# Mamba scan layer of a decoder trunk: output products for two groups at a time, and a group's scale spread by transfers through memory

## The chip, the cores and the metric

The kernel runs on one core of a Trainium2 chip. The metric is the device time of one execution, in microseconds (us). A core has five engines with an instruction queue each, which run in order and wait for each other by semaphores: PE multiplies matrices (PEld is its weight loading), DVE and ACT do element-wise work and can read PSUM, POOL does element-wise work on SBUF, SP only issues transfers. PE writes to PSUM, here eight banks of 128 x 512 floats: three "mm" banks, three "aux" and two "side".

## What is computed

A trunk of four residual layers over 512 tokens of 1024 channels, all float32: attention, a gated FFN, a Mamba-2 scan layer, and a second gated FFN. The change is in the scan layer:

```python
zxbcdt = h @ w_in                       # z, x, B, C of 8 groups, and dt
xbc = jax.nn.silu(causal_depthwise_conv(xbc, conv_w, conv_b))
y = ssd_chunked_scan(xs, dt, a, bm, cm) # per group: 4 heads of 64, state 128, chunks of 128 tokens
y = y + d_skip * xs
g = y * silu(z)                         # then per group of 256 channels:
g = g * lax.rsqrt(jnp.mean(g * g, axis=-1, keepdims=True) + NORM_EPS)
x = x + (g * norm_w) @ w_out            # 8 groups x 256 channels -> 1024
```

## The kernel before, in words

Channels lie on the partitions and the 512 tokens along a row, so an activation of 128 channels is one 128 x 512 tile. Every weight and activation is split into a high and a low part, and a product of a 128 x 128 weight tile is three matmuls (`mm3`: high by high, high by low, low by high); a "product" below is one such matmul. A weight unit is 128 x 1024 floats: a transfer brings it into a `raw` tile (four buffers), ACT casts it to `hi`, and DVE (POOL for z) subtracts to `lo`; `hi` and `lo` have five buffers each. A unit's buffers are free when PE has done its last product with them.

The scan layer goes over the eight groups g in a loop of three parts i = 0, 1, 2. While the scan of group g runs, PE fills the time with the six projections of group g+1 (x0, b, c, x1, z0, z1: 24 products each, into an mm bank, which DVE reads once, `us...<-...,rbc`, L656) and with output products for earlier groups (`write_groups`, "wso"). A scan is a generator, `scan_group`: decays; transposes and the C*B product (px, pb, pc); states (pst); products and outputs (py, pf, then yt, and on ACT the squares whose sum on DVE is `gsq`); then the norm. For the norm, PE sums the squares over the partitions (`ss`), DVE adds epsilon (`ms`, L201), POOL raises to the power -1/2 (`rg`, 128 x 4, a token's scale on its partition, L202). PE then spreads rg so that every partition has all 512 scales in a row (`along_free`, four float32 products with the identity that show as eight matmuls, tile `prg`, L209), and DVE multiplies the group's two y tiles by it (L805), ACT casts them to high (`y..h`, L807) and DVE subtracts to low (`y..l`, L809).

`write_groups(gs, ys)` makes eight steps, one for each 128 output channels m; a step is 6 products for every group in gs, summed in one mm bank, and then one DVE add into the residual tile xr[m] (L830). Before, the gs are [0,1], [2,3], [4], [5,6] and, at the end, [7].

PE's order is the order of the program here (`manual_schedule`): `between(g)` lists what fills group g's loop, `behind(g)` advances the scans, and `last_rows` writes out the end, where the first products of the next FFN (`part`) are set between the last output steps. The order on DVE, ACT, POOL and SP is made by a scheduler with its own estimate of times, and `queued(name)` ties an instruction to stand behind a given one on its engine.

Of the kernel before, what the change touches and what calls it, by code (L numbers as in the profile page):

```python
# [27 lines left out]
NSG = 8  # L28
# [9 lines left out]
C_GN = C_FIN + KD  # L38
# [13 lines left out]
def trunk(ctx: ExitStack, tc: tile.TileContext, A, out):  # L52
    nc = tc.nc
    V, SC, G, T = nc.vector, nc.scalar, nc.gpsimd, nc.tensor
    dma = nc.sync.dma_start
# [20 lines left out]
    def t2(name, tag, bufs, pool=k2, dtype=F32):  # L76
        return pool.tile([P, 512], dtype, tag=tag, name=name, bufs=bufs)
# [16 lines left out]
    rbc = cp.tile([P, S], F32, tag="rbc", name="rbc")  # L94
# [8 lines left out]
    def col(c):  # L103
        return par[:, c : c + 1]
# [100 lines left out]
    def along_free(r, name, bank=aux_bank):  # L205

        p = bank(name)
        for j in range(r.shape[-1]):
            T.matmul(  # L209
                p[:, j * P : (j + 1) * P], r[:, j : j + 1].to_broadcast([P, P]), ident,  # L210
                start=True, stop=True,
            )
        return p
# [132 lines left out]
    def qk_steps(h):  # L346
        steps = [lambda g=g, c=c: qk_step(h, g, c) for g in range(NG) for c in range(2)]
        return steps + [lambda: v0_step(h)]
# [126 lines left out]
    def wo_first(m):  # L475
        hi, lo = load_unit(A["wo"][m], f"wo{m}")
        p = mm_bank(f"wo{m}") if m < 3 or m > 4 else (aux_bank, side_bank)[m - 3](f"wo{m}")
        for h in range(NH - 1):
            mm3(p, hi, lo, h, oh[h], ol[h], h == 0, False)
        wo_held[m] = (hi, lo, p)  # L480
# [3 lines left out]
    for h in range(NH):  # L484
        if h < NH - 1:
            fill = qk_steps(h + 1)
            if h == NH - 2:
                fill.pop()
        else:
            fill = qk_steps(h)[-1:] + [lambda m=m: wo_first(m) for m in range(3)]  # L490
# [14 lines left out]
    lp = ctx.enter_context(tc.tile_pool(name="lp", bufs=1, reuse_waits="tile"))  # L505
    xr = [lp.tile([P, S], F32, tag=f"xr{k}", name=f"xr{k}") for k in range(KD)]
# [7 lines left out]
    for m in range(KD):  # L514
        if m not in wo_held:
            wo_first(m)
        hi, lo, p = wo_held[m]
# [3 lines left out]
            op=ALU.add  # L521
# [66 lines left out]
    def cst(name):  # L588
        return lp.tile([P, P], F32, tag=name, name=name)

    dtt, adt, acs, dec, cdec = (cst(n) for n in ("dtt", "adt", "acs", "dec", "cdec"))
    rows = tc.dram_tile([NSH, S], F32, name="rows")
    dt3, dec3, cd3 = c3(dtt), c3(dec), c3(cdec)

    def decay_rates():
# [51 lines left out]
    latest = {}  # L647

    def queued(name):
        return tc.issue_after(latest.pop(name).ins) if name in latest else nullcontext()  # L650

    def ssm_tile(i, c_conv, name):
        p = project(A["win"][i], name, V if c_conv is not None else G)
        us = t2("us" + name, *(("a", 13) if c_conv is None else ("us", 3)), lp)
        with queued("mean"):
            V.tensor_tensor(us, p, rbc, op=ALU.mult)  # L656
        if c_conv is None:
            with queued("decay"):
                latest["gate"] = SC.activation(us, us, AF.Silu)
            return us  # L660
        a = t2("a" + name, "a", 13, lp)
        conv(a, us, C_SCW + c_conv * 4, C_SCB + c_conv, 4)
        with queued("decay"):
            SC.activation(a, a, AF.Silu)
        return a
# [16 lines left out]
    def scan_group(g, d, ys):  # L682
# [116 lines left out]
        yield  # L799
        rg = sm.tile([P, 4], F32, tag="rg", name="rg")  # L800
        latest["mean"] = inv_rms(sq0, 2 * P, rg, bank=side_bank)
        yield
        prg = along_free(rg, "prg")
        for x, y in enumerate((y0, y1)):
            V.scalar_tensor_tensor(y, y, col(C_GN + 2 * g + x), prg, op0=ALU.mult, op1=ALU.mult)  # L805
            ys.append(high_low(f"y{g}{x}"))
            SC.copy(ys[-1][0], y)  # L807
        for y, (y_h, y_l) in zip((y0, y1), ys[-2:]):
# [4 lines left out]
    def write_groups(gs, ys):  # L813

        units = {}

        def load(i):
            if i not in units:
                units[i] = [load_unit(A["wso"][2 * g + i], f"wso{g}{i}") for g in gs]

        def step(m):
            i, at = divmod(m, 4)
            load(i)
            p = mm_bank(f"wso{gs[0]}{m}")
            n = 2 * len(gs)
            for c in range(n):
                hi, lo = units[i][c // 2]
                mm3(p, hi, lo, at * 2 + c % 2, *ys[2 * gs[0] + c], c == 0, c == n - 1)
            with queued("mean"):
                V.tensor_tensor(xr[m], xr[m], p, op=ALU.add)  # L830
            if gs[-1] == NSG - 1:
                prep(m, xr[m], C_FFN + KD, ssum_b)

        def timed(m):
            f = lambda: step(m)
            f.products = 6 * len(gs)
            return f

        return load, [timed(m) for m in range(KD)]

    ys = []
    tiles = [{} for _ in range(NSG)]
    ahead = [project_group(g, tiles[g]) for g in range(NSG)]

    w01, w23, w4, w56 = (write_groups(gs, ys)[1] for gs in ([0, 1], [2, 3], [4], [5, 6]))
    scans = [scan_group(g, tiles[g], ys) for g in range(NSG)]

    def behind(g):

        for i in range(3):  # L850
            late = g in (1, 2)
            if late and i == 2:
                next(scans[g - 1], None)
            next(scans[g])
            if g and i == (1 if late else 0) or g > 2 and i == 1:
                next(scans[g - 1], None)
            yield

    def between(g):

        if g < NSG - 1:
            x0, b, c, x1, z0, z1 = ahead[g + 1]
        if g < NSG - 3:
            after = ahead[g + 2][0]
            return [
                [[b, c], [x1, z0], [z1, after]],
                [[b, c], [x1, z0], [z1, after]],
                [[b, c], [x1, z0], [z1, after, *w01[:2]]],
                [[b, w01[2], c], [x1, w01[3], z0], [z1, after, *w01[4:6]]],
                [[b, w01[6], c], [x1, w01[7], z0], [z1, after, *w23[:2]]],  # L870
            ][g]
        if g == NSG - 3:
            return [b, w23[2], c], [x1, w23[3], z0], [z1, *w23[4:6]]
        if g == NSG - 2:
            return [x0, b], [c, x1], [z0, *w23[6:]]
        return [*w4[:4], ahead[g][5]], [*w4[4:], *w56[:2]], w56[2:4]

    def groups():
        decays = decay_rates()
        next(decays)  # L880
        for i, f in enumerate(ahead[0]):
            f()
            if i == 1:
                next(decays)
        next(decays, None)
        ahead[1][0]()
        next(scans[0])
        for g in range(NSG):
            for i, (_, fill) in enumerate(zip(behind(g), between(g))):
                for j, f in enumerate(fill):  # L890
                    f()
                    if i == 2 and j == 0 and g < NSG - 1:
                        next(scans[g + 1])

    def last_rows():

        scan = scans[-1]
        load7, w7 = write_groups([7], ys)
        next(scan)
        w56[4]()
        load7(0)
        load7(1)
        units = []

        def unit(i):
            name = f"u1_{i}"  # L910
            units.append((
                load_unit(A["wup"][44 + i], name), side_bank(name) if i in (1, 2) else mm_bank(name), name
            ))

        def part(i, *ks):
            if i == len(units):
                unit(i)
            (hi, lo), t, _ = units[i]
            for k in ks:
                mm3(t, hi, lo, k, xh[k], xl[k], k == 0, k == KD - 1)  # L920

        unit(0)
        with tc.manual_schedule(engines={mybir.EngineType.DVE, mybir.EngineType.Activation}):
            next(scan, None)
            for m in range(5, KD):
                w56[m]()
        for m in range(5):
            w7[m]()
        part(0, 0)
        w7[5]()  # L930
        part(0, 1)
        part(1, 0)
        w7[6]()
        part(0, 2)
        part(1, 1)
        part(2, 0)
        w7[7]()
        for k in range(3, KD + 2):
            for i in range(3):
                if k - i < 5:  # L940
                    part(i, k - i)
        for k in range(5, KD):
            for i in range(3):
                part(i, k)
        inv_rms(ssum_b, D, rcol)
        part(3, *range(4))
        p = along_free(rcol, "rb")
        SC.copy(rbc, p)
        part(3, *range(4, KD))
        for _, t, name in units:  # L950
            early[name] = t
# [142 lines left out]
```

## Time and profile before

| | us |
|---|---|
| median of 3 runs | 1669.96 (1669.91 to 1670.53) |
| the profiled execution | 1668.99 |
| its span, first to last instruction | 1667.2 |
| PE busy | 1648.6 |
| DVE busy | 1072.1 |
| ACT busy | 665.4 |
| POOL busy | 464.3 |
| scan layer in the span, about | 880 to 1315 |

In a timeline row the first number is the start in us from the span's start, the second the duration, then engine, line, operation, output<-inputs, the shape and how many; a bracket at the end tells how long the engine sat idle before it and who ended that. In a row of waits stand the total, how many, and the longest. Rows of the chain of waits have start, duration, engine, tile and line. In a table by stretches each engine has its busy time, with the number of instructions in brackets. Rows of transfers end with the median time from issue to landing.

### The profile page before, as it was taken

To read this page: it belongs to the slowest core of one execution; us is meant where nothing else is said; L and a number is where in the kernel's file an instruction comes from. 1 tells how busy PE (TensorE), PEld (TensorE's weight loads), DVE (VectorE), ACT (ScalarE), POOL (GpSimd) and SP (SyncE) were. 2 spreads that over 40 slices of the span, in tenths; PEclk is the share of its full clock that TensorE was granted. 3 is DMA by queue.
4 is the path that set the end of the run, shared out by engine and by line. 5 is a ranking of instruction groups with operands and counts; after the bars stand their busy time and mean duration, and the time that the engine had idled before them with its cause. 6 is when DMAs were issued, how large, how long until landed. Compare 5 with 4: busy or idle time off the path is not lost.

```text
span 1667.2 us, 21490 instructions
## 1 busy us (share of the span) xinstructions
PE 1648.6 (99%) x8230; PEld 1400.2 (84%) x8230; DVE 1072.1 (64%) x1796; ACT 665.4 (40%) x1000; POOL 464.3 (28%) x303
## 2 busy tenths in 40 slices
PE   9999999999999999999999999999989999999997
PEld 8888888888888888888888888888878888888887
DVE  5366555366658745745666888887787684574565
ACT  5233332333244423433445545454443542342345
POOL 0443443144404210220232232333230331121023
PEclk9999999999999999999999999999999999999999
DMA  7322222222223323233233333322332232332323
GB/s 252 102 77 75 82 84 89 89 76 89 76 89 127 101 88 114 90 100 101 76 114 116 102 101 102 114 75 103 101 102 78 87 113 88 102 101 89 110 74 120
DMA packets 52342, 165.56 MB, mean 99 GB/s; under 512 B 5840, under 2 KB 8144, under 8 KB 52240
## 3 DMA queue, kind: packets, MB, share of 16 engines
q1 hardware_dynamic: 51152, 163.15, 29.6%
q8 instruction: 65, 1.06, 0.3%
q10 hardware_dynamic: 1088, 1.05, 0.2%
q14 instruction: 37, 0.30, 0.1%
HBM read 162.01 MB, written 2.16 MB: 98 GB/s over the span
## 4 chain that ended last, share of the span: by engine, by line
PE 87%; DVE 7%; ACT 3%; issue 2%; DMA 1%; POOL 0%; SPq 0%; POOLq 0%; ACTq 0%; DVEq 0%
PE u L127 28%; PE qk L127 15%; PE wd L127 12%; PE v L127 8%; PE wso L127 4%; PE z L127 3%; PE xs L127 3%; PE wz L127 2%; PE wo L127 2%; DVE axs L529 1%; PE b L127 1%; PE c L127 1%; PE pp L416 1%; PE pg L429 1%; PE po L424 1%
## 5 line engine op out<-in xcount | busy, mean ns | idle before, releaser
L127 PE MATMUL u<-xl,hi_u 128*128 128x512 f32 x704 | 270.0, 384 | 0.4 <-DVE xl L176 0.4
L127 PE MATMUL u<-xh,hi_u 128*128 128x512 f32 x704 | 270.4, 384 | 0.0
L127 PE MATMUL u<-xh,lo_u 128*128 128x512 f32 x704 | 270.0, 384 | 0.0
L551 POOL TENSOR_TENSOR au<-au,au 128x512 f32<-128x512 f32 x43 | 56.7, 1320 | 427.0 <-DVE au L529 406.4
L118 ACT CAST hi_u<-raw_u 128x1024 fp32r<-128x1024 f32 x88 | 91.1, 1043 | 193.9 <-PE u L127 102.1
L529 DVE SCALAR_TENSOR_TENSOR au<-usu,par,au 128x510 f32<-128x510 f32 (+1 forms) x176 | 160.8, 918 | 5.9 <-ACT au L527 1.0
L331 POOL TENSOR_TENSOR rotqk<-rotqk,sr 32x512 f32<-32x512 f32 x48 | 91.9, 1914 | 258.1 <-DVE rotqk L330 215.0
L127 PEld LDWEIGHTS u<-xl,hi_u 128*128 128x128 f32 x704 | 131.9, 187 | 25.9 <-DVE xl L176 0.8
L127 PEld LDWEIGHTS u<-xh,lo_u 128*128 128x128 f32 x704 | 131.9, 187 | 25.4
L127 PEld LDWEIGHTS u<-xh,hi_u 128*128 128x128 f32 x704 | 131.9, 187 | 25.2
L127 PE MATMUL qk<-xh,hi_qk 128*128 128x512 f32 x384 | 149.3, 389 | 0.0
L127 PE MATMUL qk<-xl,hi_qk 128*128 128x512 f32 x384 | 148.4, 387 | 0.0
L127 PE MATMUL qk<-xh,lo_qk 128*128 128x512 f32 x384 | 147.2, 383 | 0.0
L544 DVE TENSOR_TENSOR usu<-u,rbc 128x512 f32<-128x512 f32 x88 | 60.5, 690 | 113.3 <-PE u L127 103.9
L119 DVE TENSOR_TENSOR lo_u<-raw_u,hi_u 128x1024 fp32r<-128x1024 f32 x88 | 110.8, 1264 | 24.2 <-ACT hi_u L118 24.2
L564 DVE TENSOR_TENSOR xr<-xr,wd 128x512 f32<-128x512 f32 x40 | 27.3, 687 | 116.8 <-PE wd L127 116.8
L327 DVE TENSOR_TENSOR qk<-qk,cr 128x512 f32<-128x512 f32 x48 | 33.0, 688 | 91.5 <-PE qk L127 91.3
L118 ACT CAST hi_qk<-raw_qk 128x1024 fp32r<-128x1024 f32 x48 | 50.2, 1045 | 100.4 <-PE v L127 50.0
L127 PEld LDWEIGHTS qk<-xh,lo_qk 128*128 128x128 f32 x384 | 72.0, 187 | 13.4
L127 PEld LDWEIGHTS qk<-xh,hi_qk 128*128 128x128 f32 x384 | 72.0, 188 | 13.0
L118 ACT CAST hi_wd<-raw_wd 128x1024 fp32r<-128x1024 f32 (+1 forms) x56 | 52.3, 952 | 76.7 <-PE wd L127 39.7
L127 PEld LDWEIGHTS qk<-xl,hi_qk 128*128 128x128 f32 x384 | 72.1, 188 | 12.5
(636 smaller groups left out, 3931.1 us busy)
## 6 DMA issues: line engine op xcount, KB each, us to landing
raw_u<-in_wup SPq DMA_DIRECT2D x88, 512.0 KB, 3.2
raw_qk<-in_wqk SPq DMA_DIRECT2D x48, 512.0 KB, 3.2
raw_wd<-in_wdn SPq DMA_DIRECT2D x32, 512.0 KB, 3.2
raw_wd<-in_wdn SPq DMA_DIRECT2D x24, 384.0 KB, 2.9
raw_xs<-in_win SPq DMA_DIRECT2D x16, 512.0 KB, 3.3
raw_z<-in_win SPq DMA_DIRECT2D x16, 512.0 KB, 3.6
lm<-rows SPq DMA_DIRECT2D x32, 256.0 KB, 5.9
raw_wso<-in_wso SPq DMA_DIRECT2D x16, 512.0 KB, 3.2
```

The source lines that it names most:

```text
L118: SC.copy(hi[:, s], raw[:, s])
L119: low.tensor_tensor(lo[:, s], raw[:, s], hi.bitcast(F32)[:, s], op=ALU.subtract)
L127: T.matmul(in_turns(dst), w, in_turns(x), start=first, stop=last)
L327: V.tensor_tensor(at(t), of(p), of(cr), op=ALU.mult)
L331: G.tensor_tensor(rot[R, :], rot[R, :], sr[R, :], op=ALU.mult)
L416: T.transpose(pp[:, b * P : (b + 1) * P], pr[:, b * P : (b + 1) * P], ident)
L424: T.matmul(po[:, ii], v0[h][:, b * P : (b + 1) * P], pts[i][:, (b - i + 1) * P : (b - i + 2) * P], start=b == max(i - 1, 0), stop=b == i,)
L429: T.matmul(pg[:, ii], vt[g, half][i][:, es], pts[i][:, (g + 1) * P : (g + 2) * P], start=g == 1, stop=g == 2,)
L529: V.scalar_tensor_tensor(dst[:, j:], src[:, : S - j], col(c_w + taps - 1 - j), dst[:, j:], op0=ALU.mult, op1=ALU.add,)
L544: V.tensor_tensor(us, p, rbc, op=ALU.mult)
L551: by.tensor_tensor(ab[1], ab[0], ab[1], op=ALU.mult)
L564: V.tensor_tensor(xr[m], xr[m], p, op=ALU.add)
```

## The change

Output steps take two groups throughout: [0,1], [2,3], [4,5], and [6,7] at the end; the steps of [4] and [7] alone (6 products) and of [5,6] are gone. The places of the steps in the last loops move with that: two of [2,3] move from loop 6 to loop 7, and loop 7 has three steps of [4,5] in part 1 and two in part 2, with the rest in `last_rows`.

For the groups 0 to 6, rg no longer goes over PE. A transfer from SP writes its 128 x 4 values to a row of `scales` in DRAM in the order of tokens (element by element: neighbours in the row come from neighbouring partitions), and a second transfer reads the row back to all 128 partitions as `prg` in SBUF. The second waits for the first. Group 7 still uses `along_free`. The sum of squares `ss` moves in groups 0 and 1 from behind the states to behind the C*B product, as it already stood for the later groups. The multiplication by the scale (L813 after) is tied on DVE to stand behind the last copy or add made before it in the program.

```diff
+    scales = tc.dram_tile([NSG, S], F32, name="scales")
...
         latest["mean"] = inv_rms(sq0, 2 * P, rg, bank=side_bank)
-        yield
-        prg = along_free(rg, "prg")
+        if g < NSG - 1:
+            dma(scales[g].rearrange("(j t) -> t j", t=P), rg)
+            prg = t2("prg", "prg", 1, lp)
+            dma(prg, scales[g : g + 1, :].to_broadcast([P, S]))
+            yield
+        else:
+            yield
+            prg = along_free(rg, "prg")
         for x, y in enumerate((y0, y1)):
-            V.scalar_tensor_tensor(y, y, col(C_GN + 2 * g + x), prg, op0=ALU.mult, op1=ALU.mult)
+            with queued("copy"):
+                V.scalar_tensor_tensor(y, y, col(C_GN + 2 * g + x), prg, op0=ALU.mult, op1=ALU.mult)
...
-    w01, w23, w4, w56 = (write_groups(gs, ys)[1] for gs in ([0, 1], [2, 3], [4], [5, 6]))
+    w01, w23, w45 = (write_groups(gs, ys)[1] for gs in ([0, 1], [2, 3], [4, 5]))
...
         if g == NSG - 3:
-            return [b, w23[2], c], [x1, w23[3], z0], [z1, *w23[4:6]]
+            return [b, c], [x1, w23[2], z0], [z1, *w23[3:5]]
         if g == NSG - 2:
-            return [x0, b], [c, x1], [z0, *w23[6:]]
-        return [*w4[:4], ahead[g][5]], [*w4[4:], *w56[:2]], w56[2:4]
+            return [x0, b], [c, x1], [z0, w23[5]]
+        return [*w23[6:], ahead[g][5]], w45[:3], w45[3:5]
...
-            for i, (_, fill) in enumerate(zip(behind(g), between(g))):
+            for i, fill in enumerate(between(g)):
+                next(scans[g])
+                if g and i == 0:
+                    next(scans[g - 1])
                 for j, f in enumerate(fill):
                     f()
+                    if g and i == 1 and j == 0:
+                        next(scans[g - 1], None)
...
-        load7, w7 = write_groups([7], ys)
+        load67, w67 = write_groups([6, 7], ys)
         next(scan)
-        w56[4]()
-        load7(0)
-        load7(1)
+        w45[5]()
+        load67(0)
...
-            for m in range(5, KD):
-                w56[m]()
-        for m in range(5):
-            w7[m]()
+            for m in range(6, KD):
+                w45[m]()
+        for m in range(4):
+            w67[m]()
```

Three places of the new order are used below, all on DVE. Names carry the group or step and a buffer number; the change adds 8 to L830 (L838) and to L805, L807 and L809 (L813, L815, L817), and 1 to the lines between.

Loop 3, between the norm's `ms` of group 2 and the projection c of group 4, before:

```order
L201 TENSOR_SCALAR ms_8336<-ss_8331 128x4
L656 TENSOR_TENSOR usb4_8370<-b4_8345,rbc_98 128x512
L529 SCALAR_TENSOR_TENSOR ab4_8372<-usb4_8370,par_76,ab4_8372 128x511
L529 SCALAR_TENSOR_TENSOR ab4_8372<-usb4_8370,par_76,ab4_8372 128x510
L830 TENSOR_TENSOR xr2_4044<-xr2_4044,wso02_8378 128x512
L529 SCALAR_TENSOR_TENSOR ab4_8372<-usb4_8370,par_76,ab4_8372 128x509
L656 TENSOR_TENSOR usc4_8423<-c4_8398,rbc_98 128x512
```

and after:

```order
L201 TENSOR_SCALAR ms_8333<-ss_8328 128x4
L657 TENSOR_TENSOR usb4_8370<-b4_8345,rbc_98 128x512
L529 SCALAR_TENSOR_TENSOR ab4_8372<-usb4_8370,par_76,ab4_8372 128x511
L529 SCALAR_TENSOR_TENSOR ab4_8372<-usb4_8370,par_76,ab4_8372 128x510
L838 TENSOR_TENSOR xr2_4044<-xr2_4044,wso02_8378 128x512
L529 SCALAR_TENSOR_TENSOR ab4_8372<-usb4_8370,par_76,ab4_8372 128x509
L813 SCALAR_TENSOR_TENSOR yt_8141<-yt_8141,par_76,prg_8337 128x512
L657 TENSOR_TENSOR usc4_8423<-c4_8398,rbc_98 128x512
```

The first multiplication by the scale now stands ahead of the reading of c's bank (usc4); before, it stood six rows behind it.

Loop 7, from the squares' sum of group 6 to its `ms`, before:

```order
L798 TENSOR_TENSOR gsq_9864<-gsq_9864,gsq_9871 128x512
L119 TENSOR_TENSOR lo_wso41_10123<-raw_wso41_10121,hi_wso41_10122 128x1024
L732 TENSOR_SCALAR lm_9909<-lm_9909,acs_6861 128x128 x3
L830 TENSOR_TENSOR xr6_4048<-xr6_4048,wso26_9942 128x512
L732 TENSOR_SCALAR lm_9911<-lm_9911,acs_6861 128x128 x3
L732 TENSOR_SCALAR lm_9914<-lm_9914,acs_6861 128x128 x3
L732 TENSOR_SCALAR lm_9916<-lm_9916,acs_6861 128x128 x3
L119 TENSOR_TENSOR lo_wso50_10161<-raw_wso50_10159,hi_wso50_10160 128x1024
L830 TENSOR_TENSOR xr7_4049<-xr7_4049,wso27_9956 128x512
```

and after:

```order
L799 TENSOR_TENSOR gsq_9839<-gsq_9839,gsq_9846 128x512
L838 TENSOR_TENSOR xr5_4047<-xr5_4047,wso25_9917 128x512
L694 TENSOR_TENSOR xdt_9936<-px_9931,dtt_6859 128x512
L733 TENSOR_SCALAR lm_9884<-lm_9884,acs_6861 128x128 x3
L733 TENSOR_SCALAR lm_9886<-lm_9886,acs_6861 128x128 x3
L694 TENSOR_TENSOR xdt_9951<-px_9946,dtt_6859 128x512
```

Between z0 of group 7 and `ss` of group 6 PE has one output step now (wso25), where it had two (wso26, wso27).

The end of the scan layer, from the last outputs of group 7 to its `ms`, before:

```order
L766 TENSOR_TENSOR yt_10232<-yt_10232,usz71_10079 128x512
L830 TENSOR_TENSOR xr2_4044<-xr2_4044,wso52_10240 128x512
L798 TENSOR_TENSOR gsq_10230<-gsq_10230,gsq_10237 128x512
L119 TENSOR_TENSOR lo_wso71_10311<-raw_wso71_10309,hi_wso71_10310 128x1024
L830 TENSOR_TENSOR xr3_4045<-xr3_4045,wso53_10254 128x512
L201 TENSOR_SCALAR ms_10274<-ss_10269 128x4
```

and after:

```order
L767 TENSOR_TENSOR yt_10157<-yt_10157,usz71_10033 128x512
L119 TENSOR_TENSOR lo_wso70_10236<-raw_wso70_10234,hi_wso70_10235 128x1024
L838 TENSOR_TENSOR xr3_4045<-xr3_4045,wso43_10165 128x512
L119 TENSOR_TENSOR lo_u1_0_10242<-raw_u1_0_10240,hi_u1_0_10241 128x1024
L799 TENSOR_TENSOR gsq_10155<-gsq_10155,gsq_10162 128x512
L838 TENSOR_TENSOR xr4_4046<-xr4_4046,wso44_10191 128x512
L201 TENSOR_SCALAR ms_10211<-ss_10206 128x4
```

Two low parts of weight units and an add stand ahead of the squares' sum now, where one add stood. Both units take over the buffers of units whose last product is step wso43.

On SP the two transfers of a scale stand between weight loads; for group 2 the load of wso11 is right behind them. On POOL the four products of decays and C*B (`lm`, L794 before) of the loop all stand ahead of `rg` in loops 1 to 5; in loop 3 before, three of them did.

More of the change, by code (lines that the diff above doesn't have):

```diff
@@ L655, in ssm_tile @@
         with queued("mean"):
-            V.tensor_tensor(us, p, rbc, op=ALU.mult)
+            latest["copy"] = V.tensor_tensor(us, p, rbc, op=ALU.mult)
         if c_conv is None:
@@ L829, in step @@
             with queued("mean"):
-                V.tensor_tensor(xr[m], xr[m], p, op=ALU.add)
+                latest["copy"] = V.tensor_tensor(xr[m], xr[m], p, op=ALU.add)
             if gs[-1] == NSG - 1:
@@ L843, in trunk @@
     ahead = [project_group(g, tiles[g]) for g in range(NSG)]
-    w01, w23, w4, w56 = (write_groups(gs, ys)[1] for gs in ([0, 1], [2, 3], [4], [5, 6]))
+    w01, w23, w45 = (write_groups(gs, ys)[1] for gs in ([0, 1], [2, 3], [4, 5]))
     scans = [scan_group(g, tiles[g], ys) for g in range(NSG)]
[L848 to L857, printed above, removed]
     def between(g):
@@ L924, in last_rows @@
             next(scan, None)
-            for m in range(5, KD):
-                w56[m]()
-        for m in range(5):
-            w7[m]()
+            for m in range(6, KD):
+                w45[m]()
+        for m in range(4):
+            w67[m]()
         part(0, 0)
-        w7[5]()
+        w67[4]()
         part(0, 1)
         part(1, 0)
-        w7[6]()
+        w67[5]()
         part(0, 2)
         part(1, 1)
+        w67[6]()
+        part(0, 3)
+        part(1, 2)
         part(2, 0)
-        w7[7]()
+        w67[7]()
         for k in range(3, KD + 2):
             for i in range(3):
-                if k - i < 5:
+                if k - i < 6 and (k > 3 or i == 2):
                     part(i, k - i)
-        for k in range(5, KD):
+        for k in range(6, KD):
             for i in range(3):
```

## The prediction

> **What bounds the kernel now.** I read the page first, then PE by stretches of the scan layer, then what PE waited for there.
>
> ```profile
> span 1667.2 us, 21490 instructions
> ...
> PE 1648.6 (99%) x8230; PEld 1400.2 (84%) x8230; DVE 1072.1 (64%) x1796; ACT 665.4 (40%) x1000; POOL 464.3 (28%) x303
> ```
>
> PE is busy in 99% of the span, so work taken off PE counts in full, work taken off another engine only where PE waits for it, and a new wait counts only if it reaches PE.
>
> ```profile
> 1030.00:1080.00 50.00, 50.00 (x278) 42.71 (x277) 42.95 (x73) 24.02 (x35) 13.68 (x9) 1.00 0.34 111
> ```
>
> After the stretch come PE, PEld, DVE, ACT and POOL. In loop 3, from 1030 to 1080, PE never stops, and DVE is busy for 42.95 of 50. Then PE's waits from 930 to 1330, and one of them in the timeline:
>
> ```profile
> PE wso L127 <- DVE xr L830: 6.0, 4, 2.3
> PE prg L209 <- POOL rg L202: 2.1, 3, 1.0
> ```
> ```profile
> 1245.60 0.49 PE L127 MATMUL wso<-y40h,hi_wso 128*128 128x512 f32 x1 [2.32 <-DVE xr L830]
> ```
>
> There are no others. Four times an output step waited until DVE had added an earlier one into xr and so freed its bank (the longest, 2.32, ahead of a 6-product step of group 4, y40h). Three times the spreading of a scale waited for POOL.
>
> **The change part by part.** The next rows, of the chain of waits, give the prices on PE, in loop 3.
>
> ```profile
> 1043.27 0.79 PE ss L196 x8
> 1044.05 5.52 PE b L127 x24
> 1049.58 2.68 PE wso L127 x12
> 1052.26 5.36 PE c L127 x24
> 1057.62 1.34 PE pst L704 x12
> 1058.95 0.89 PE prg L209 x8
> ...
> 1094.94 0.79 PE ss L196 x8
> ```
>
> *Removed.* Seven of eight prg are gone: 7 x 0.89 = 6.2 us. The waits in front of them go too: 2.1 us. The steps of 6 products become steps of 12 (2.68 us), the same products in all, so PE gains nothing there, but one add (0.7 us of DVE, as its other 128 x 512 rows) now serves 12 products, and the 6.0 us of waits go. Together -14.3 us. Eight adds fewer on DVE lie beside PE's work and count as nothing in themselves.
>
> *Added: the way through memory.* The trace has no such pair. These are the nearest rows:
>
> ```profile
> out<-ot SPq DMA_DIRECT2D x4, 256.0 KB, 2.7
> ...
> rows<-ar SPq DMA_DIRECT2D x1, 64.0 KB, 1.6
> par<-in_par SPq DMA_DIRECT2D x1, 8.0 KB, 1.8
> ```
> ```profile
> DMA to landing us min/median/max: 5.0/5.9/7.1
> ```
>
> The write is 512 pieces of 4 bytes. A write of 32 rows took 1.6 us, a load of 128 short rows 1.8: if 96 pieces more cost 0.2 us, 512 cost 1.8 + 384 x 0.2/96 = 2.6 us. It can't be below 1.6; if time went wholly with pieces it would be 4 x 1.8 = 7.2. I take 2.6, since 1.6 and 1.8 show a fixed part that dominates. The read is 256 KB from one row: 2.7 us for a lone transfer of that size, 5.0 for the fastest of the lm transfers (the second fence), which read rows in the same way but go out in fours; I take 3.0. With 0.1 to issue, 5.7 us, and between 4.3 and 12.2.
>
> What waits for it is DVE, at the first multiplication (L813). The rows of DVE in loop 3, then of POOL:
>
> ```profile
> 1050.35 0.15 DVE L201 TENSOR_SCALAR ms<-ss 128x4 f32<-128x4 f32 x1
> ...
> 1055.06 1.17 DVE L529 SCALAR_TENSOR_TENSOR ab<-usb,par,ab 128x509 f32<-128x509 f32 x1
> 1057.65 0.69 DVE L656 TENSOR_TENSOR usc<-c,rbc 128x512 f32<-128x512 f32 x1 [1.42 <-PE c L127]
> ```
> ```profile
> 1050.97 4.71 POOL L794 TENSOR_TENSOR lm<-lm,cb 128x512 f32<-128x512 f32 x3
> 1055.63 1.46 POOL L202 TENSOR_TENSOR rg<-ms,mhalf 128x4 f32<-128x4 f32 x1
> 1057.07 1.28 POOL L794 TENSOR_TENSOR lm<-lm,cb 128x512 f32<-128x512 f32 x1
> ```
>
> The fourth lm goes ahead of rg now, so rg ends at 1055.63 + 1.28 + 1.46 = 1058.4 and the scale lands at 1058.4 + 5.7 = 1064.1. DVE reaches L813 at 1056.2, behind the last ab: it stands still for 7.9 us. Queued behind it are usc (which frees the bank of c), the prev rows that pf needs, the conv of c, and ACT's casts. For the bank: usc ends at 1064.1 + 0.7 + 0.7 = 1065.5. Three mm banks rotate, so c's is wanted again by z0, after pst, xs (5.4) and a step (2.7): at 1044.05 + 5.5 + 2.7 + 5.4 + 1.3 + 5.4 + 2.7 = 1067.0. So 1.5 us to spare. In loop 5 the step between b and c is gone, which takes 2.7 away, and its wait is 1.2 us. DVE has no room: 42.95 + 7.9 = 50.9 us of work and standing in a loop that takes PE 50.8 (51.7, from ss to ss, less 0.89). So DVE falls no further behind, but does not catch up either. For loops 3 to 5 together I put +2.0. In loops 1 and 2 L813 stands behind usc, so no bank hangs on it: nothing. If the cover were gone, each loop would cost PE up to the 7.9.
>
> *Added: SP.* SP waits for rg and for the landing of the write. Behind the pair in loop 3 stands the load of wso11.
>
> ```profile
> 1045.21 15.82 SPq L114 DMA_DIRECT2D raw_wso<-in_wso  x2
> ```
>
> It went out last at about 1061 already (it waits for a buffer); now the pair leaves SP free at about 1061.4. Its first product comes after xs, a step, z, z and xs, some 25 us later. Nothing.
>
> *Moved: the squares' sum of group 6 (loop 7).* PE now has one step fewer ahead of ss, and no prg with its wait:
>
> ```profile
> 1206.37 1.16 PE L209 MATMUL prg<-ident,rg 128*128 128x128 f32 x8 [0.44 <-POOL rg L202]
> ...
> 1234.35 0.95 PE L196 MATMUL ss<-ones,gsq 128*128 128x1 f32 x8
> ```
> ```profile
> 1233.27 0.69 DVE L798 TENSOR_TENSOR gsq<-gsq 128x512 f32<-128x512 f32 x1
> ```
>
> ss would be reached 2.7 + 0.9 + 0.4 = 4.0 us earlier, at 1230.4 on the old clock. But gsq ended only at 1233.96, behind a stretch in which DVE and ACT were full; L813 stands in that stretch too, and I suppose that the multiplications and the add taken out of it make up for that. I keep 1233.96: PE waits 3.5 us.
>
> *Moved: the squares' sum of group 7 (the end).* Before, on PE, DVE and ACT:
>
> ```profile
> 1269.67 5.36 PE wso L127 x24
> 1275.03 0.79 PE ss L196 x8
> ```
> ```profile
> 1271.76 0.69 DVE L766 TENSOR_TENSOR yt<-yt,usz 128x512 f32<-128x512 f32 x1
> 1272.39 0.69 DVE L830 TENSOR_TENSOR xr<-xr,wso 128x512 f32<-128x512 f32 x1
> 1273.15 0.69 DVE L798 TENSOR_TENSOR gsq<-gsq 128x512 f32<-128x512 f32 x1
> 1274.63 1.23 DVE L119 TENSOR_TENSOR lo_wso<-raw_wso,hi_wso 128x1024 fp32r<-128x1024 f32 x1 [0.79 <-ACT hi_wso L118]
> ```
> ```profile
> 1272.48 0.63 ACT L768 ACTIVATE gsq<-yt 128x512 f32<-128x512 f32 x1 [0.56 <-DVE yt L766]
> 1273.55 1.05 ACT L118 CAST hi_wso<-raw_wso 128x1024 fp32r<-128x1024 f32 x1 [0.43 <-PE wso L127]
> ```
>
> gsq was done 1.2 us before ss. Now, from the end of pf (where the 24 products begin): step wso43 ends at 2.7 and frees two weight buffers; ACT casts, with the squares between (0.6 each), to 3.8 and 5.5; DVE does lo_wso70 to 5.1, xr3 to 5.7, lo_u1_0 to 7.0, gsq to 7.7. PE reaches ss at 5.4. PE waits 2.4 us. Behind ss nothing else opens: steps of 12 give DVE 2.7 us for an add and a split (0.7 + 0.7). Only step wso61, whose bank hangs on an add behind a low part, may cost 0.4.
>
> *Sum.* -14.3 + 2.0 + 3.5 + 2.4 + 0.4 = -6.0 us, on 1668.99 us (the profiled execution, 1.8 us over its span): 1663.0. The median is 1.0 us above that execution: 1664.0.
>
> **The rivals.**
>
> *The transfers are slow (slower than before).* One mechanism: L813 holds DVE longer than the spare time, usc frees c's bank late, and PE stops before z0 in loops 3, 4 and 5 and before ss in loop 7. Past 5.7 us each microsecond more costs up to 4. At 7.2 us for the pair the gain is gone, at 8.0 the kernel is slower by 0.2%; with 8.5 it is -6.0 + 4 x 2.8 = +5.2: 1675. For it: 512 pieces, and a DVE without slack. Against it: the small fixed times above. The Trainium skill speaks for it ("DMA: Bandwidth & Descriptors", Rules for kernel authors): a non-contiguous last dimension lowers to one descriptor per element, and transposing by a plain rearranged transfer is a 19-fold loss. No run so far shows a price for such a piece.
>
> *All is hidden.* The ss waits don't come, because DVE, freed of eight adds, runs ahead: -14.3 + 1 = -13.3, 1656.7. For it: the chain through DVE ended in the 6-product steps. Against it: the two new places in DVE's order.
>
> *The waits only move (no change).* The 6.0 us of bank waits come back in full in the last two loops, beside the new waits at ss, since DVE and ACT set the pace there whatever the length of a step: -6.0 + 6.0 = 0, 1670.0. For it: DVE at its limit. Against it: the adds that are fewer fall just there.
>
> **How the numbers follow.** The forecast has 0.55, slow transfers 0.15, all hidden 0.13, moved waits 0.17. A measurement can tell about 0.2%, 3.3 us. Of the forecast's 0.55, whose own range is 1660 to 1668, some 0.08 lies within 3.3 us of before; with all hidden, faster is 0.60. Same is 0.17 + 0.08 = 0.25, slower 0.15. The range, 1657 to 1673, holds the forecast and the moved waits, half of the hidden case and the nearer part of the slow one (a pair of up to 8 us); the far bound of 12.2 us is left out.
>
> **What would show it.** PE's wait prg <- POOL rg should be left at most for group 7, wso <- xr near zero, and ss should have waited for gsq by about 3.5 us (loop 7) and 2.4 us (the end). DVE's wait for prg should be near 8 us in loops 3 to 5, and under 2 in loops 1 and 2. The transfers should show 2.6 and 3.0 us. I am wrong if PE waits at z0 for usc (the bank) by more than 2 us in all, if ss doesn't wait, or if a weight load comes late.

## The result and the profile after

The changed kernel takes 1737.16 us (median; 1736.63 to 1738.89), the kernel before, run beside it, 1670.05 us (1669.91 to 1670.53). The ratio is 1.0403, with a 95% interval of 1.0385 to 1.0421. The change makes the kernel slower by 67 us, where 6 us of gain were forecast; the range ended at 1673. The profiled execution took 1736.63 us, with a span of 1734.8.

From the page of the changed kernel, the span, the busy times and the chain that ended last:

```profile
span 1734.8 us, 21398 instructions
...
PE 1660.1 (96%) x8174; PEld 1408.7 (81%) x8174; DVE 1052.7 (61%) x1788; ACT 665.4 (38%) x1000; POOL 463.3 (27%) x303
...
PE 81%; DMA 6%; DVE 5%; issue 3%; POOL 2%; ACT 2%; SPq 0%; POOLq 0%; ACTq 0%; DVEq 0%
```

PE is no longer busy in 99% of the span but in 96%, and 6% of the last chain are transfers. The two new ones, in the list of DMA issues (last column: median us from issue to landing):

```profile
prg<-scales SPq DMA_DIRECT2D x7, 256.0 KB, 5.5
...
scales<-rg SPq DMA_DIRECT2D x7, 2.0 KB, 8.0
```

By these medians the pair takes 13.5 us, where 5.7 were forecast and 12.2 was the far bound. The longest write, in loop 7, took 10.8 us. What PE waited for in the scan layer (us in total, times, longest), and two lines of the same view for DVE and SP:

```profile
PE pf L752 <- DVE prev L714: 27.5, 3, 11.5
PE z L127 <- DVE usc L657: 24.7, 3, 9.9
PE wso L127 <- DVE usz L657: 6.2, 1, 6.2
PE px L692 <- ACT axs L665: 4.1, 1, 4.1
PE ss L196 <- DVE gsq L799: 2.2, 2, 1.5
```
```profile
DVE yt L813 <- DMA prg<-scales: 96.5, 7, 16.4
```
```profile
SPq L806 <- DMA scales<-rg: 55.7, 7, 9.8
```

DVE stands 96.5 us at the multiplications, 13.8 per group: 9.7 us each in loops 1 and 2, about 16 each in loops 3 to 5, 14 each in loops 6 and 7. In loops 3, 4 and 5 this reaches PE as the wait of z for usc (the bank, as the prediction had it), in loops 1, 2 and 6 as the wait of pf for prev, which the prediction didn't have. Loop 1 on DVE:

```profile
976.24 0.28 DVE L710 TENSOR_TENSOR prev<-prev,cdec 128x128 f32<-128x128 f32 x1
986.27 0.75 DVE L813 SCALAR_TENSOR_TENSOR yt<-yt,par,prg 128x512 f32<-128x512 f32 x1 [9.74 <-DMA prg<-scales]
...
989.92 0.47 DVE L714 TENSOR_TENSOR prev<-prev,pst 128x128 f32<-128x128 f32 x2
...
990.92 0.74 DVE L813 SCALAR_TENSOR_TENSOR yt<-yt,par,prg 128x512 f32<-128x512 f32 x1
```

One multiplication of the two stands in the middle of the prev rows and waits 9.74 us with them behind it; the other stands behind usxs and finds the scale there. The reason is in the code: `queued("copy")` takes its entry out of the table when it is used, so that only the first multiplication in the program (y0) is tied behind the latest copy. The second (y1) is free, and in the order it stands earlier.

PE's busy time grew by 11.5 us, although 6.2 us of spreads are gone. The windows around the stop of loop 1 show why (width of the slice, then PE, PEld, DVE, ACT, POOL; the granted clock is the third column from the right):

```profile
978.00:980.00 2.00, 0.72 (x14) 0.48 (x10) 0.00 (x0) 0.00 (x0) 0.00 (x0) 1.00 0.00 0
...
982.00:984.00 2.00, 0.00 (x0) 0.00 (x0) 0.00 (x0) 0.00 (x0) 0.00 (x0) 0.61 0.02 8
984.00:986.00 2.00, 0.00 (x0) 0.00 (x0) 0.00 (x0) 0.00 (x0) 0.00 (x0) 0.50 0.60 240
...
994.00:996.00 2.00, 2.00 (x7) 1.52 (x6) 1.97 (x4) 0.15 (x1) 0.00 (x0) 0.50 0.96 287
996.00:998.00 2.00, 2.00 (x10) 1.73 (x9) 2.00 (x4) 1.17 (x2) 0.00 (x0) 0.97 0.89 213
```
```profile
990.25 2.93 PE L752 MATMUL pf<-ac,prev 128*128 128x128 f32 x12 [11.53 <-DVE prev L714]
```

PE falls idle at 978.7. The granted clock goes to 0.50 at about 982.4 and comes back at about 996.1, 5.8 us after PE started again at 990.25. The products behind the stop run at half speed until then. The Trainium skill ("TensorE: Matmul & The Clock Gate", Why this matters for your kernels) says to leave no gap of more than about 3 us between bursts of products, or the clock falls to half; the trace agrees, with 3.7 us here.

In the stretch from 880 to 1400, before and after:

```profile
880.00:1400.00 520.00, 511.90 (x2716) 434.13 (x2715) 405.39 (x658) 245.74 (x352) 146.69 (x96) 1.00 0.30 99
```
```profile
880.00:1400.00 520.00, 455.22 (x2354) 384.76 (x2353) 336.63 (x598) 216.22 (x315) 122.53 (x81) 0.93 0.31 90
```

PE is idle for 64.8 us there, before for 8.1: 56.7 more. Busy share times lost clock, summed over slices of 1 us, is another 19.1. Less the 6.2 us of spreads, that is 69.6, against 67.6 of span: the account closes to 2 us. It is a sum of where PE's time goes, not of independent causes, as the filled stops below show.

### The profile page after: what moved, and what is told of

Same layout as the page of the kernel before. It is cut to its first block, busy times and chain, and to the rows that moved or that the text cites. A ratio compares the mean times of both kernels' runs of the same rounds, so it can differ in the third digit from the quotient of the medians.

```text
span 1734.8 us, 21398 instructions
## 1 busy us (share of the span) xinstructions
PE 1660.1 (96%) x8174; PEld 1408.7 (81%) x8174; DVE 1052.7 (61%) x1788; ACT 665.4 (38%) x1000; POOL 463.3 (27%) x303
## 2 busy tenths in 40 slices
DMA packets 57045, 167.40 MB, mean 96 GB/s; under 512 B 9648, under 2 KB 11952, under 8 KB 56944
## 3 DMA queue, kind: packets, MB, share of 16 engines
q8 instruction: 64, 1.05, 0.2%
q10 hardware_dynamic: 1088, 1.05, 0.2%
## 4 chain that ended last, share of the span: by engine, by line
PE 81%; DMA 6%; DVE 5%; issue 3%; POOL 2%; ACT 2%; SPq 0%; POOLq 0%; ACTq 0%; DVEq 0%
PE u L127 27%; PE qk L127 15%; PE wd L127 12%; PE v L127 7%; DMA scales<-rg 3%; PE z L127 3%; PE wso L127 3%; DMA prg<-scales 2%; PE xs L127 2%; PE wz L127 2%; PE wo L127 1%; POOL lm L795 1%; PE b L127 1%; PE pp L416 1%; PE pg L429 1%
## 5 line engine op out<-in xcount | busy, mean ns | idle before, releaser
L551 POOL TENSOR_TENSOR au<-au,au 128x512 f32<-128x512 f32 x43 | 56.7, 1318 | 427.0 <-DVE au L529 406.3
```

The costliest lines, as they stand in the source:

```text
L551: by.tensor_tensor(ab[1], ab[0], ab[1], op=ALU.mult)
```

## The experiments

All ratios are to the kernel before in the same set of runs (medians of 1668.5 to 1669.9 us there). The main theory: the loss is DVE standing at the multiplications until the pair has landed, with work behind it that PE needs; the regrouping itself gains a little. The rivals: the regrouping or the new places do the harm; or the transfers do it by themselves, by contention or by occupying SP.

**The regrouping alone.** The edit: `prg = along_free(rg, "prg")` in place of the two transfers, for all groups.

> The regrouped output steps and the new places of the squares' sums without any transfer: every scale is spread on PE as before. Theory (the loss sits in the transfers' latency, the regrouping itself gains a little): the bank waits before output steps (6.0 us) go, the squares' sums wait about 2.2 us as in the changed kernel, the seven spreads stay: 1664 to 1669 us, and PE's granted clock stays at 1.00. Rival (the regrouping or the earlier places of the scale in loops 1 and 2 bring the stops): 1700 us or more, with the long waits of pf and z still there.

Measured: 1667.09 us, ratio 0.9986 (0.9976 to 0.9995). PE's waits:

```profile
PE ss L196 <- DVE gsq L798: 2.3, 2, 1.3
PE py L743 <- DVE prev L713: 1.6, 1, 1.6
PE prg L209 <- POOL rg L202: 0.4, 1, 0.4
```

The bank waits of 6.0 us are gone, as forecast, and those of prg fell from 2.1 to 0.4. PE's idle time is 4.7 us instead of 8.1, but 3.4 us go to a lower clock behind the two waits of ss, so PE's account of the scan layer doesn't explain the gain. By the ratio the regrouping is worth 2.3 us (0.8 to 4.0) and does no harm.

**The transfers alone.** The edit: the two transfers in the kernel before, groups 0 to 6, no ties.

> The kernel before with its old grouping of the output steps; only the scales of groups 0 to 6 go through memory, in pieces of 4 bytes. Theory (the loss is DVE standing at the multiplications until the pair has landed, whatever the grouping): in loops 3 to 6 both multiplications stand ahead of usc and wait 6 to 12 us, PE stops at z or pf, its clock falls after each stop, and the time is 1700 to 1730 us. Rival (the pair hurts only together with the regrouped steps, which took the cover away): under 1690 us.

Measured: 1760.2 us, ratio 1.0544 (1.0529 to 1.0558), worse than the whole change and past the range the theory gave. Loop 3 on DVE:

```profile
1098.94 1.42 DVE L812 SCALAR_TENSOR_TENSOR yt<-yt,par,prg 128x512 f32<-128x512 f32 x2 [17.38 <-DMA prg<-scales]
1100.38 0.69 DVE L816 TENSOR_TENSOR y20l<-yt,y20h 128x512 fp32r<-128x512 f32 x1
1101.04 0.69 DVE L816 TENSOR_TENSOR y21l<-yt,y21h 128x512 fp32r<-128x512 f32 x1
1101.65 0.68 DVE L657 TENSOR_TENSOR usc<-c,rbc 128x512 f32<-128x512 f32 x1
```

Both multiplications and both low parts stand ahead of usc, and z waits 12 us in each of three loops. The old bank waits stay too (6.9 us). The rival (harm only together with the regrouping) falls. The write took 9.4 us at the median here: the runs with 512 pieces differ in this, 8.0 in the changed kernel and 8.5 to 9.6 in the others, so small differences between their totals are not to be relied on.

**The changed kernel without its tie.** The edit: the multiplication without `with queued("copy")`.

> The changed kernel without the tie of the first multiplication: neither multiplication by the scale is held behind a copy. Grouping, transfers and the places on PE are the changed kernel's. Theory (what the loss grows with is the work that stands on DVE ahead of usc and prev and hangs on the scale): both multiplications and the low parts behind them stand there, PE's stops become 10 to 14 us as in the run of the transfers alone, and the time is 1748 to 1765 us. Rival (the free second multiplication alone sets the wait, so the tie gains nothing): 1733 to 1742 us.

Measured: 1749.77 us, ratio 1.0488 (1.0473 to 1.0503). The stops are 14.4, 12.1, 6.2, 10.4, 11.3 and 10.7 us. So the tie of the first multiplication, half a tie, is worth about 0.85% or 14 us; up to some 4 us of this may be the write, which took 8.5 us here against 8.0.

**Both multiplications tied.** The edit:

```diff
+        copy = latest["copy"].ins
         for x, y in enumerate((y0, y1)):
-            with queued("copy"):
+            with tc.issue_after(copy):
```

> The changed kernel, with one line more: the tie that holds a group's first multiplication by the scale behind the latest copy (usxs) holds the second one too; in the changed kernel the second one is free and stands on DVE ahead of prev and usc. Transfers, their queue and their number are the same. Theory (the loss is the place at which DVE stands, not the transfers): the stops of PE at pf and z go, DVE still stands some 6 us per group at L813 behind usxs, which PE mostly does not feel: 1662 to 1678 us, clock back near 1.00. Rival (the transfers themselves, by contention or by the queue they occupy, slow the kernel): still above 1715 us.

Measured: 1704.33 us, ratio 1.0205 (1.0189 to 1.0220). This is far outside the theory's range. The stops of pf and z are gone as the theory has it, and half of the loss with them. But DVE still stands 46.7 us, behind usxs now, and I had thought that PE would mostly not feel it:

```profile
978.80 0.69 DVE L657 TENSOR_TENSOR usxs<-xs,rbc 128x512 f32<-128x512 f32 x1
986.36 1.41 DVE L814 SCALAR_TENSOR_TENSOR yt<-yt,par,prg 128x512 f32<-128x512 f32 x2 [6.88 <-DMA prg<-scales]
```
```profile
PE ss L196 <- DVE gsq L799: 10.2, 3, 6.5
PE wso L127 <- DVE usz L657: 8.3, 4, 4.6
PE pb L778 <- DVE yt L763: 6.2, 2, 3.7
```

What is late next is usz, yt and gsq: in this run DVE's wait was handed on to whatever stands behind it.

**Both tied, one projection later.** The edit, on top: `if g and i == 1 and j == len(fill) - 1`, so that the latest copy is usz0.

> As the run with both multiplications tied, and both come one projection later, behind the copy of z0, some 8 us after usxs. Theory: the scale has then landed when DVE arrives, DVE's wait for prg falls from 96.5 us to under 15, PE's waits at pf and z are zero, and the time is 1658 to 1666 us, faster than before. Rival (the pair of transfers costs by itself): above 1700 us. Rival (DVE has no room later in the loop either): slower than the run with both tied.

Measured: 1685.2 us, ratio 1.0091 (1.0076 to 1.0106). This too is outside the theory's range (1658 to 1666), and under the rival's 1700: with the same transfers on the same queue the loss fell from 4.0% to 0.9%, so contention and the occupied SP can account for no more than this rest. DVE's wait for the scale is down to 6.9 us, and between 1047 and 1234 PE has no stop of over 0.3 us. What is left lies at the two ends of the scan layer:

```profile
1244.34 1.87 PE L196 MATMUL ss<-ones,gsq 128*128 128x1 f32 x8 [7.38 <-DVE gsq L799]
```
```profile
ACT hi_wso L118 <- DMA raw_wso<-in_wso: 9.5, 2, 5.0
```

In loops 1 and 2 DVE still stands 3 us each for the scale. In loop 7 ss waited 7.4 us for gsq; DVE worked without a pause from the late multiplications of group 5 (at 1225.2) to gsq (until 1244.3). The second fence is no cause of it: SP stands some 9 us between the two transfers, and two weight loads behind it came late, but at 1082 and 1132, where PE has no stop.

**The write in 128 pieces of 16 bytes.** The edit, with the changed kernel's order on DVE:

```diff
-            dma(scales[g].rearrange("(j t) -> t j", t=P), rg)
+            dma(scales[g].rearrange("(t j) -> t j", j=4), rg)
```

and prg read through "p (t j) -> p j t".

> The changed kernel with its order on DVE, but the scale is written in 128 pieces of 16 bytes instead of 512 of 4, and DVE reads the broadcast scale with a stride of four elements. Theory (the write's time goes with its pieces): the write takes 2 to 3 us instead of about 8, the pair about 8 instead of 13.5, DVE stands about 5.5 us less per group (96.5 to about 58 us in all), and the time falls to 1685 to 1705 us. Rival (a fixed latency, whatever the pieces): the write still takes 7 us or more and the time stays within 5 us of 1737.

Measured: 1690.75 us, ratio 1.0125 (1.0110 to 1.0140).

```profile
prg<-scales SPq DMA_DIRECT2D x7, 256.0 KB, 4.6
...
scales<-rg SPq DMA_DIRECT2D x7, 2.0 KB, 1.4
```
```profile
PE pf L752 <- DVE prev L714: 7.6, 4, 3.3
PE z L127 <- DVE usc L657: 4.3, 2, 3.5
```
```profile
L815 DVE SCALAR_TENSOR_TENSOR yt<-yt,par,prg x16: 739/1186/1229, 977.4 to 1294.0; 128x512 f32<-128x512 f32 x16
```

The write falls from 8.0 to 1.4 us, and DVE's wait for the scale from 96.5 to 42.9. With the pair at 6.0 us, nearly the 5.7 that I had reckoned with, this run shows what else the prediction missed: the kernel is still 27 us above the 1664 that the sum gave. PE is idle for 24.4 us of the stretch from 880 to 1400, and busy share times lost clock is another 13.0. By the third fence a part of the 27 us is this run's own: with the strided operand the multiplication takes 1.19 us (median) instead of 0.75, which makes up to 14 x 0.44 = 6 us of DVE.

**What the write's price goes by.** Two runs: 256 pieces of 8 bytes (rearranged as "(a t b) -> t a b"; the scales then reach other columns, which leaves the work the same), and four transfers of 128 pieces of 4 bytes, one per column of rg.

> The changed kernel with the scale written in 256 pieces of 8 bytes. The rows then land in another order than DVE reads them, so the scales reach other columns: the output isn't the reference's, the work is the same. Theory (the write's time goes with the number of pieces beyond some 128: 1.4 us for 128, 8.0 for 512, so 17 ns a piece): about 3.6 us for the write, and a time a third of the way from 1690.8 (pieces of 16) to 1737.2: 1700 to 1712 us. Rival (short pieces are slow as such, whatever their number): 6 us or more for the write and over 1722 us.

> The changed kernel with the scale written by four transfers, one per column of rg, each of 128 pieces of 4 bytes that land side by side in memory. Theory (the number of pieces decides): 512 pieces are in flight all the same, so the last of the four lands 7 to 10 us after the first was issued, and the time is within 8 us of 1737 or above. Rival (what costs is that the pieces of one transfer land 512 bytes apart): each of the four takes 1.5 to 3 us, SP stands 4 us instead of 8, and the time is below 1720 us.

Measured: 1699.2 us, ratio 1.0186 (1.0169 to 1.0203), 0.8 us under the theory's range, and 1743.99 us, ratio 1.0449 (1.0433 to 1.0465).

```profile
scales<-rg SPq DMA_DIRECT2D x7, 2.0 KB, 3.3
```
```profile
972.06 1.75 SPq L805 DMA_DIRECT2D scales<-rg  x4
981.30 0.32 SPq L807 DMA_DIRECT2D prg<-scales  x1
```

128, 256 and 512 pieces took 1.4, 3.3 and 8.0 us. In the run by columns (second fence) the read, which waits for all four writes, went out 9.2 us after the first of them, though the pieces of a column land side by side. So the price doesn't go by the distance at which the pieces land. It goes with their number, by these medians 15 to 18 ns for each piece beyond 128. As every run writes the same 2 KB, more pieces are also shorter ones, and these runs can't tell the number from the shortness; per piece, 256 of 8 bytes cost 13 ns and 512 of 4 bytes 16. The Trainium skill ("DMA: Bandwidth & Descriptors", Rules for kernel authors) had spoken against a rearranged transfer that lowers to one descriptor per element; these runs agree: against the 9648 packets of under 512 bytes in the changed kernel, the run with 256 pieces has 7 x 256 fewer and that with 128 pieces 7 x 384 fewer, one for each piece that is saved.

**Late, in pieces of 16.** The two edits together.

> The run with both multiplications tied behind the copy of z0 (1685.2 us), with the scale written in 128 pieces of 16 bytes. Theory (what is left of the loss is still the write's time: DVE's wait in loop 1, and SP, which stands some 10 us between the two transfers with weight loads queued behind it): the pair takes about 8 us, SP stands some 5 us less, DVE's wait for prg goes, and the time falls to 1666 to 1677 us. Rival (the late multiplications themselves delay gsq at the end of the loop): still above 1681 us.

Measured: 1679.85 us, ratio 1.0060 (1.0047 to 1.0074), 3 us outside the theory's range. DVE doesn't wait for a scale now, and ACT for no weight load. The gain over the run before it is 5 us, and in the traces it lies mainly in loops 1 and 2, where DVE stood. But PE's waits at ss are no shorter (11.6 us before this edit):

```profile
PE ss L196 <- DVE gsq L799: 12.6, 3, 6.3
```

Most of what is left fits the rival: at the two ends of the scan layer the late multiplications push gsq itself back. Before the last ss, for instance, DVE works without a pause from the multiplications of group 6 at 1260.3 to gsq, which ends at 1272.5.

**The hybrid.** Regrouped steps; only the scales of groups 1 to 3 go through memory (16 bytes, tied, late), the others are spread on PE at their earlier place.

> Regrouped output steps; the scales of groups 1, 2 and 3 alone go through memory, in pieces of 16 bytes, with their multiplications tied behind the copy of z0; those of groups 0 and 4 to 7 are spread on PE. Theory (in loops 2 to 4 the late place costs PE nothing, and the two ends of the scan layer are where DVE has no room): 3 x 0.9 us less than the regrouping alone (1667.1): 1662 to 1666 us. Rival (the pair costs something wherever it stands): 1668 us or more.

Measured: 1663.51 us, ratio 0.9966 (0.9952 to 0.9979).

```profile
PE ss L196 <- DVE gsq L799: 2.3, 2, 1.3
PE pf L752 <- DVE prev L714: 1.5, 1, 1.5
```

This is 0.34% (0.21 to 0.48) below the kernel before, the first version with a scale through memory to be faster than it. No wait for a scale is left on DVE, and PE is idle for 5.1 us of the stretch from 880 to 1400, against 4.7 with the regrouping alone. Two variants:

> The hybrid (groups 1 to 3 through memory, late; 1663.5 us) with the squares' sum of group 6 one output step later on PE in loop 7, so that gsq is done when PE comes to it. Theory: the wait of 1.3 us there and the lowered clock behind it go, and nothing behind needs the scale earlier: 1660.5 to 1663 us. Rival (group 6's scale is then late for its output steps): 1664 us or more.

> The hybrid with group 4 through memory as well (groups 1 to 4, late). Theory (loop 5 has room like loops 2 to 4): 0.9 us less than the hybrid: 1661.5 to 1663.5 us. Rival (in loop 5, which has one output step fewer, DVE's backlog reaches gsq or px in loop 6): 1665 us or more.

Measured: 1662.84 us, ratio 0.9964 (0.9951 to 0.9976), and 1663.08 us, ratio 0.9967 (0.9956 to 0.9978). Neither can be told from the hybrid. In the first the wait at the moved ss went, and a wait of 0.9 us for rg came at prg; in the second the spread saved isn't seen in the time.

**The stops filled.** Products that serve nothing, into pf's bank ahead of pf, to keep the clock up. First try:

> The changed kernel with products that serve nothing put on PE ahead of pf in loops 1, 2 and 6 (30, 30 and 16 of 128x512, into pf's own bank, which pf overwrites), where PE stood 11.5, 9.6 and 6.3 us. Nothing else moves. Theory (PE's granted clock falls to a half some 3 us into a stop and comes back some 5 us after it): the filled stops leave less than 5 us of idleness each, the clock stays up there, the products behind run at full speed, and the kernel with 76 products more is 4 to 8 us faster: 1729 to 1733 us. Rival (the low clock has another cause, such as the transfers or the small products): no faster than 1736 us.

Measured: 1754.34 us, ratio 1.0508 (1.0493 to 1.0522). Stops of 5.9, 6.5 and 4.6 us were left, the pf rows behind them still took 2.93 to 3.03 us, and the wait of wso for usz in loop 7 grew from 6.2 to 14.5: there the write went out only 4.1 us before PE came to that step, where it had been 10.5, and the pair took 2 us longer. The writes were slower throughout this run (9.5 us at the median), and DVE stood 111.8 us for the scale. The run decides nothing on the clock. Second try:

> The changed kernel with 46 products of 128x512 that serve nothing ahead of pf in loop 1 and 38 in loop 2 (10.3 and 8.5 us), none in loop 6: enough that at most some 3 us of each stop are left, where the first try left 5.9 and 6.5. Theory (the clock falls only in a stop of more than about 3 us): the granted clock stays at 1.00 through both places and the work behind them gains some 2.5 us each, against some 1 us lost where the products overrun. Rival (the clock falls for another reason): it is near 0.50 behind both places as before. The place in the trace decides, more than the total (1730 to 1740 us by the theory).

Measured: 1744.84 us, ratio 1.0486 (1.0432 to 1.0541), so not faster. The place in loop 1, then the one in loop 2:

```profile
978.83 10.72 PE L753 MATMUL pf<-xh 128*128 128x512 f32 x46
990.40 1.60 PE L755 MATMUL pf<-ac,prev 128*128 128x128 f32 x12 [0.84 <-DVE prev L714]
```
```profile
990.00:994.00 4.00, 3.60 (x22) 3.27 (x23) 4.00 (x8) 3.96 (x6) 0.00 (x0) 1.00 0.06 6
```
```profile
1044.28 2.93 PE L755 MATMUL pf<-ac,prev 128*128 128x128 f32 x12 [3.34 <-DVE prev L714]
```

With 0.8 us left of the stop the clock stays at 1.00, and pf takes 1.60 us instead of 2.93. In loop 2, where 3.3 us were left, the clock fell to 0.50 just before PE started again, and pf took 2.93 us. That the stop itself lowers the clock is shown. That the clock costs the kernel 19 us is not: PE began the next ss in loop 1 1.5 us earlier, but POOL came to rg 1.2 us later than in the changed kernel, so the next scale was written at 1026.28 instead of 1025.09, and pf of loop 2 came at 1044.28 instead of 1042.54. In this loop the chain through DVE, POOL and the transfers set the pace, and faster products only waited longer. Part of the rise in the total may be the write, 8.5 us here against 8.0, with DVE standing 100.7 us instead of 96.5; the rest stays open.

## Why the prediction was wrong

The direction was wrong, and the time lay far outside the range. By its own steps:

- *PE bounds the kernel, and a new wait counts only if it reaches PE*: right. 56.7 us of waits reached it.
- *Removed, -14.3 us*: the waits did go. In the run of the regrouping alone the bank waits are zero and the prg waits 0.4. But new waits of ss, py and px (4.3 us) and the clock behind them (3.4) took back as much as these two terms gave there (7.7), and the run gained 2.3 us against its neighbours. The 6.2 us of spreads it kept.
- *The write, 2.6 us*: wrong, 8.0 measured. This is the first step that failed. I drew a line through two rows that differ by 96 pieces and 0.2 us, par and rows, and let a fixed part of about 1.6 us dominate. The runs give 15 to 18 ns per piece beyond 128: the line was eight times too flat. The bound 4 x 1.8 = 7.2, time wholly with pieces, was the nearer of my two.
- *The read, 3.0 us*: wrong, 5.5. The lm transfers, the very same pattern, had 5.0 as their fastest; I put them aside because they go out in fours. A lone read of this pattern took 4.6 us even in the run with the short write.
- *The bank of c in loops 3 to 5, +2.0*: right but for the price. With the measured pair, 7.8 us longer than reckoned, the same reckoning (1.5 us to spare in loops 3 and 4, 1.2 of wait in loop 5) gives 6.3, 6.3 and 9.0 us; measured were 7.0, 7.8 and 9.9. DVE's own waits come out as well: 7.9 + 7.8 = 15.7, measured 15.9 to 16.4. Of the 2.0, only the 1.2 of loop 5 was worked out.
- *"In loops 1 and 2 L813 stands behind usc, so no bank hangs on it: nothing"*: wrong, the second step that failed. I had listed the prev rows as queued behind L813 and then priced only the bank. PE's pf waits for prev; loops 1, 2 and 6 cost 27.5 us, more than loops 3 to 5, and loop 6 I hadn't priced at all. The run with a pair of 6.0 us shows what this step, the clock and other waits missed cost together with nearly my own prices for the pair: 1690.8 us instead of 1664, of which up to 6 us are the strided operand's; pf's own waits are 7.6 there.
- *"DVE falls no further behind"*: wrong as far as it was to mean that its wait is harmless. With both multiplications behind usxs, DVE stood 6.7 us a group, about what I had reckoned, and PE was idle for 32 us of the scan layer instead of 8, mostly at ss, usz, pb and px.
- *SP, nothing*: right; in the scan layer ACT never waited for a weight load. In the run with both tied late it waited 9.5 us for two, but where PE had no stop.
- *The squares' sums, 3.5 and 2.4 us*: the right places, with 0.7 and 1.5 us. That PE itself came later to them is likely, but no run tests it.
- *The granted clock*: no step had it, the third that failed. It was 1.00 in the rows I quoted, and I took the price of a stop for its length. By the account above it is 19.1 us of PE's time here, and 13.0 beside 24.4 of idleness in the run with the short write; how much of it the kernel would get back at full clock isn't shown.

The rival of slow transfers named the mechanism and got 0.15. With the measured 13.5 us its rule of 4 us per microsecond gives -6.0 + 4 x 7.8 = +25, or 1695 us. It too counted only usc's bank and ss; pf (27.5 us), usz (6.2) and axs (4.1) were missing. "All hidden" and "the waits only move" fall; the waits that moved to ss were small. Of the signs named beforehand, z's wait for usc, 24.7 us where more than 2 was to show me wrong, came true.

## What to carry to other kernels

Price a transfer by its number of contiguous pieces first, and if a line through two rows must serve as the price, ask what happens when the larger count is far outside them. Before costing a new wait at nothing, list every row queued behind it on its engine and follow each to the instruction on the bounding engine that needs it, loop by loop; one that hangs on no bank can still hang on data. A long wait was cheap here only where the order put it behind work that covered it, and a tie in the program may hold only one of the two rows that need it.

## What the runs showed of the hardware that I had not expected

- A write of 2 KB from 128 partitions took 1.4, 3.3 and 8.0 us in 128, 256 and 512 pieces, and up to 9.6 us (median of a run) for the 512.
- PE's granted clock fell to 0.50 after 3.7 us of idleness and stayed there for 5.8 us of work after it; in loop 2 of the second filled run it fell after 3.3 us and came back after 3.1 us of work. A shorter stop can come before a fall too: in the regrouped kernel, a wait of 1.3 us and then eight 128x1 products (the squares' sum, 1.05 us) were followed by these slices:

```profile
1228.00:1232.00 4.00, 2.73 (x16) 2.23 (x15) 3.64 (x7) 3.92 (x7) 0.83 (x1) 0.85 0.44 135
1232.00:1236.00 4.00, 4.00 (x15) 3.27 (x14) 4.00 (x14) 3.47 (x7) 1.11 (x2) 0.72 0.00 0
```

  The same wait and products in the hybrid (at 1226.5) left the clock at 1.00, and so did the waits of 2.2 and 2.3 us in the kernel before. What decides between them stays open.

- A DVE multiplication of 128x512 with one operand read at a stride of 16 bytes took 1.19 us instead of 0.75.
